# Feed-forward entry of a two-batch encoder layer: operand sums formed before the transpose instead of after it

## The chip, the cores and the metric

One core of a Trainium2 chip runs the whole layer for both batches in one launch. The metric is the device time of that launch in microseconds (us). The kernel before takes 1795.2 us (median of 3 runs, 1794.31 to 1796.43).

The engines named below: TensorE (PE in the profile) does matrix products and, by a product with an identity, transposes; VectorE (DVE), ScalarE (ACT) and GpSimd (POOL) work element by element; SyncE (SP) issues the transfers between the chip's memory (DRAM) and SBUF. TensorE writes into PSUM, which GpSimd does not read here. Each engine works through its own instructions in order.

## The reference, cut to what matters

Two batches of 512 tokens with 1024 features go through one layer: a mixer of two branches, an output projection `w_out` added to `x`, and then a feed-forward block. The change touches the seam between the projection and the feed-forward block:

```
x = x + (g_a * y_a + g_b * y_b) @ w_out[l]
h = _rmsnorm(x, norm_ffn_g[l])            # x * rsqrt(mean(x*x) + eps) * gain
gt, up = jnp.split(h @ w_gu[l], 2, axis=-1)
x = x + (jax.nn.silu(gt) * up) @ w_down[l]
```

All is float32. A product is made of three matmuls over a high and a low part: `hi*hi + hi*lo + lo*hi`, where `hi` is the value rounded to TensorE's short format and `lo` is the rest.

## The kernel before, in words

**The gate/up product.** `h @ w_gu` is done for both batches together by a scheme of seven products in place of eight (Strassen's, in Winograd's form). The transposed normalized rows are cut into four quadrants: the first and the second half of the features, for batch 0 (B11 and B21) and for batch 1 (called z0 and z1 in the code; z1 is B22). From them come the sums T1 = z0 - B11, T2 = B22 - T1, T3 = B22 - z0 and T4 = B21 - T2. The operands of the products are B11, B21, B22, T1, T2, T3 and T4, each held as a `hi` and a `lo` tile with features on the partitions. The weights of block `j` come in two loads of 512 KB, `graw` (A11 and A12) and `uraw` (A21 and A22); GpSimd forms the sums S1 to S4 from them, and ScalarE (`hi`) and VectorE (`lo`) split them. Both loads go into three shared buffers tagged `raw`.

**The order of the stages at this seam.**

1. `combine(1, ...)` makes the merged rows of batch 1, eight steps `j` with two products `pab` of 12 matmuls each. At steps 0, 2, 4 and 6 a hook calls `first_norm(t)` for row tile `t` (128 tokens) of batch 0: square and sum, the power -1/2 on GpSimd, scale the rows, transpose both halves on TensorE (`nt_f`), multiply with the gain while leaving PSUM (`nscf`), then `split` into B11 and B21. The gain stands per partition here, since the features are on the partitions after the transpose. `EF` puts the low part of this split on GpSimd.
2. `project(1, 0, ...)` multiplies with the first half of `w_out`'s columns (`pwo`).
3. A `Window` records operations with an engine, a cost, a rank and what they wait for, and writes them out in the order that its planner finds; later scheduling keeps that order. Recorded are: `w_project(t)` (second half of the columns, 24 matmuls for a row tile), `w_norm(t)` (norm, two transposes, gain, and T1, B22, T3 and T2 for batch 1), `w_combos(t)` (T2, T4 and T3 split), and `w_product(i)`, the first product and half of the next for weight blocks 0 and 1 (`pgA`).
4. `gate_up(j)` for the blocks: in block 0 and 1 `pgB` needs T1 whole, `pgC` T2 and then T3, `pgB` again B22, and `pgC` last T4.

In the window before the change a row tile's chain is: add the projection to `x` (L1447, VectorE), square and sum over 1024 features (L1457, ScalarE), L1459 (VectorE), power (L1461, GpSimd), scale 1024 features (L1462, VectorE), two transposes (TensorE), two multiplications by the gain out of PSUM (L1471, VectorE), two subtractions for T1 (L1479 and L1481: B11 exists only as `hi` and `lo`), T3 (L1485), T2 (L1487), T4 (L1494, L1495) and the splits of L1429 (ScalarE) and L1430 (GpSimd or VectorE, by the strings `ET1` to `ET4` and `EB22`).

Of the kernel before, what the change touches and what calls it, by code (L numbers as in the profile page):

```python
# [108 lines left out]
def trunk(ctx, tc, outs, x, w_in, w2, g2, w_uq, w_ukk, w_ukv, w_oab, w_out, w_gu, w_down,  # L109
          cols, fng, ident, te, to, mask2, reset, blk64, blk2):  # L110
# [1167 lines left out]
    B11, B21 = (operand(bp0, n) for n in ("B11", "B21"))  # L1278

    def first_norm(cp_, t):  # L1280
# [10 lines left out]
        for g, dst in enumerate((B11, B21)):  # L1291
            nc.vector.tensor_scalar_mul(h[g], xs[:, g], ss[:, 0:1])
# [3 lines left out]
            nc.vector.tensor_mul(sc, ps.rearrange("p (k t) -> p k t", k=KH),  # L1296
                                 cc(C_GFFN + g * KH, KH).unsqueeze(2).to_broadcast([P, KH, P]))
# [126 lines left out]
    COST = {nc.vector: ("V", 0.6), nc.gpsimd: ("G", 1.23)}  # L1424
    early, psb = {}, []

    def w_split(dst, t, src, rank, eng, *deps):
# [1 line left out]
        hi = W.op("A", 0.52, rank, lambda: nc.scalar.copy(dst()[0][:, :, ts], src()), *deps)  # L1429
        lo = W.op(*COST[eng], rank, lambda: eng.tensor_sub(dst()[1][:, :, ts], src(), dst()[0][:, :, ts]), hi)  # L1430
# [19 lines left out]
    def w_norm(t, old):  # L1450

        ts, xt, z = slice(t * P, (t + 1) * P), x2[4 + t], {}

        def square():
            z["ss"] = np_.tile([P, 1], F32, tag="nss", bufs=4, name=f"nssf1{t}")
            z["ht"] = np_.tile([P, D], F32, tag="nh", bufs=1, name=f"nhf1{t}")
            return nc.scalar.activation(z["ht"], xt, AF.Square, accum_out=z["ss"])  # L1457
        o = W.op("A", 1.04, 0, square, *psb[-1:], *old.get("tr", ()))
        o = W.op("V", 0.07, 0, lambda: nc.vector.tensor_scalar(z["ss"], z["ss"], 1.0 / D, RMS_EPS,  # L1459
                                                               op0=ALU.mult, op1=ALU.add), o)  # L1460
        o = W.op("G", 0.46, 0, lambda: nc.gpsimd.tensor_tensor(z["ss"], z["ss"], mhalf[:, :1], op=ALU.pow), o)  # L1461
        o = W.op("V", 0.66, 0, lambda: nc.vector.tensor_scalar_mul(z["ht"], xt, z["ss"]), o)  # L1462
        r = {"tr": [], "nsc": [], "z": z}

        def tr(g):
            z["ps", g] = bank(3, f"nt_f1{t}{g}")
            tr4(z["ps", g], lambda i: z["ht"][:, (g * 4 + i) * P:(g * 4 + i + 1) * P])

        def scale(g):
            z[g] = np_.tile([P, KH, P], F32, tag=f"nsc{g}", bufs=(4, 1)[g], name=f"nscf1{t}{g}")  # L1470
            return nc.vector.tensor_mul(z[g], z["ps", g].rearrange("p (k t) -> p k t", k=KH),  # L1471
                                        cc(C_GFFN + g * KH, KH).unsqueeze(2).to_broadcast([P, KH, P]))
        for g in range(2):
            r["tr"].append(W.op("T", 0.43, 0, lambda g=g: tr(g), o, *old.get("nsc", [])[g:g + 1]))
            r["nsc"].append(W.op("V", 0.6, 0, lambda g=g: scale(g), r["tr"][g], *(old.get("b22", ()) if g else ())))
# [375 lines left out]
```

## Time and profile before

| | |
|---|---|
| time, median of 3 runs | 1795.2 us (1794.31 to 1796.43) |
| the profiled execution's own time | 1793.97 us |
| its span in the trace | 1792.2 us |
| mean granted TensorE clock | 0.984 |

The page of the profile gives each engine's busy time over the span and cuts the span in 40 slices; a table of stretches gives the same for any piece of it. The list of waits says which engine stood idle for which; a timeline row gives start, duration, engine, line, operation, and in brackets the idle time just ahead of it with what ended it. A row on a line or a group gives minimum, median and maximum of its instructions' durations in ns. The seam that is changed lies between 1017 and 1173 us of the span. The rows themselves stand in the prediction, where they are used.

### The profile page before, as it was taken

To read this page: it belongs to the slowest core of one execution; us is meant where nothing else is said; L and a number is where in the kernel's file an instruction comes from. 1 tells how busy PE (TensorE), PEld (TensorE's weight loads), DVE (VectorE), ACT (ScalarE), POOL (GpSimd) and SP (SyncE) were. 2 spreads that over 40 slices of the span, in tenths; PEclk is the share of its full clock that TensorE was granted. 3 is DMA by queue.
4 is the path that set the end of the run, shared out by engine and by line. 5 is a ranking of instruction groups with operands and counts; after the bars stand their busy time and mean duration, and the time that the engine had idled before them with its cause. 6 is when DMAs were issued, how large, how long until landed. Compare 5 with 4: busy or idle time off the path is not lost.

```text
span 1792.2 us, 30028 instructions
## 1 busy us (share of the span) xinstructions
PE 1700.9 (95%) x11276; PEld 1327.8 (74%) x11276; DVE 1075.6 (60%) x1773; ACT 787.9 (44%) x1533; POOL 627.3 (35%) x984
## 2 busy tenths in 40 slices
PE   7999999999999997999999999699999999989997
PEld 6778766777777775666667877488888888868886
DVE  6734464636445365855566665955565465498657
ACT  6643424344433335666663432433333333245445
POOL 1121536274554736261012143833343333200006
PEclk9999999999999998999999999899999999999999
DMA  5473342434334344211267531123222222383442
GB/s 179 135 259 100 107 116 79 132 86 125 114 85 121 84 116 118 73 40 34 110 207 266 176 126 36 36 88 107 94 93 96 83 90 76 100 307 110 130 134 94
DMA packets 181233, 208.90 MB, mean 117 GB/s; under 512 B 102816, under 2 KB 106272, under 8 KB 181088
## 3 DMA queue, kind: packets, MB, share of 16 engines
q1 hardware_dynamic: 180224, 205.48, 36.3%
q8 instruction: 88, 1.44, 0.3%
q10 hardware_dynamic: 720, 0.98, 0.2%
q0 software_dynamic: 144, 0.52, 0.1%
q14 instruction: 57, 0.47, 0.1%
HBM read 147.70 MB, written 59.24 MB: 115 GB/s over the span
## 4 chain that ended last, share of the span: by engine, by line
PE 72%; DVE 9%; POOL 6%; DMA 6%; issue 3%; ACT 2%; SPq 1%; DVEq 0%; POOLq 0%; ACTq 0%
PE pgC L129 10%; PE pj_gt L129 8%; PE pgB L129 6%; PE pgA L129 6%; PE pj_rkv L129 4%; PE dx L129 4%; PE pwo L129 4%; PE pab L129 3%; PE s L129 2%; PE dy L129 2%; POOL el L966 2%; POOL lt L964 2%; PE sc L129 2%; PE pj_mla L129 2%; PE pav L129 2%
## 5 line engine op out<-in xcount | busy, mean ns | idle before, releaser
L964 POOL TENSOR_TENSOR lt<-lane,el 128x126 f32<-128x126 f32 (+22 forms) x248 | 94.1, 379 | 36.7 <-DMA lane<-nt_d 18.1
L966 POOL TENSOR_TENSOR el<-el,lt 128x126 f32<-128x126 f32 (+22 forms) x248 | 98.9, 399 | 19.0
L129 PE MATMUL pab<-yo,wab 128*128 128x512 f32 x384 | 96.5, 403 | 5.5 <-DVE wab L137 2.8
L129 PE MATMUL pj_gt<-h_hi,wlo_gt 128*128 128x512 f32 x240 | 98.4, 410 | 1.2 <-DVE wlo_gt L137 1.2
L129 PE MATMUL pj_gt<-h_lo,whi_gt 128*128 128x512 f32 x240 | 99.4, 414 | 0.0
L129 PE MATMUL pj_gt<-h_hi,whi_gt 128*128 128x512 f32 x240 | 99.0, 412 | 0.0
L129 PEld LDWEIGHTS pab<-yo,wab 128*128 128x128 f32 x384 | 71.7, 191 | 24.2 <-DVE wab L137 5.1
L1344 POOL TENSOR_TENSOR s<-uraw 128x512 f32<-128x512 f32 x22 | 29.3, 1334 | 154.3 <-DMA uraw<-in_w_gu 154.0
L129 PE MATMUL pwo<-woh,m 128*128 128x512 f32 x256 | 80.4, 390 | 0.0
L129 PE MATMUL pj_rkv<-h_hi,wlo_rkv 128*128 128x512 f32 x192 | 79.1, 412 | 0.0
L129 PE MATMUL pj_rkv<-h_hi,whi_rkv 128*128 128x512 f32 x192 | 78.6, 410 | 0.0
L129 PE MATMUL pj_rkv<-h_lo,whi_rkv 128*128 128x512 f32 x192 | 78.2, 407 | 0.0
L1720 POOL TENSOR_TENSOR x<-x,dp 128x512 f32<-128x512 f32 x4 | 6.3, 1593 | 177.5 <-DVE x L1719 177.5
L1412 DVE TENSOR_TENSOR p<-p,pgC 128x512 f32<-128x512 f32 x22 | 15.1, 687 | 82.3 <-PE pgC L129 82.3
L1053 ACT COPY sva<-s 64x128 f32<-64x128 f32 x64 | 16.5, 258 | 100.8 <-PE s L129 87.3
L129 PEld LDWEIGHTS pwo<-woh,m 128*128 128x128 f32 x256 | 48.1, 188 | 10.0
L1054 DVE COPY svb<-s 64x128 f32<-64x128 f32 x64 | 18.9, 295 | 60.5 <-ACT sva L1053 35.8
L775 DVE TENSOR_REDUCE mx<-sc 128x1 f32<-128x512 f32 x64 | 43.6, 687 | 15.7 <-PE sc L129 14.9
L129 PEld LDWEIGHTS pj_gt<-h_hi,wlo_gt 128*128 128x128 f32 x240 | 45.1, 188 | 9.9 <-DVE wlo_gt L137 1.7
L129 PEld LDWEIGHTS pj_gt<-h_hi,whi_gt 128*128 128x128 f32 x240 | 45.1, 188 | 8.9
L129 PEld LDWEIGHTS pj_gt<-h_lo,whi_gt 128*128 128x128 f32 x240 | 45.1, 188 | 8.6
L1354 POOL TENSOR_TENSOR s<-graw,uraw 128x512 f32<-128x512 f32 x22 | 29.2, 1325 | 63.8 <-DVE S_2l L137 5.0
(1563 smaller groups left out, 5458.4 us busy)
## 6 DMA issues: line engine op xcount, KB each, us to landing
graw<-in_w_gu SPq DMA_DIRECT2D x22, 512.0 KB, 3.6
uraw<-in_w_gu SPq DMA_DIRECT2D x22, 512.0 KB, 3.6
a_d<-a SPq DMA_DIRECT2D x21, 512.0 KB, 3.4
w<-in_w_down SPq DMA_DIRECT2D x42, 256.0 KB, 4.5
x<-in_x SPq DMA_DIRECT2D x16, 512.0 KB, 7.1
rwkv_in<-lut SPq DMA_DIRECT2D x32, 256.0 KB, 2.4
gate_d<-gtt SPq DMA_DIRECT2D x32, 256.0 KB, 2.4
wab<-in_w_oab SPq DMA_DIRECT2D x32, 256.0 KB, 3.8
```

Source lines behind the costliest of these rows:

```text
L129: pin(nc.tensor.matmul(out, lhsT, rhs, start=start, stop=stop, **kw), n if out.shape[0] > 64 else n / 2)
L775: nc.vector.tensor_reduce(mx, sc, axis=AX.X, op=ALU.min)
L964: eng.tensor_mul(lv, lane[:, s, s + 1:].unsqueeze(1).to_broadcast([P, m_, n]), el[:, 0:m_, s].unsqueeze(2).to_broadcast([P, m_, n]))
L966: eng.tensor_add(ev, ev, lv)
L1053: nc.scalar.copy(sva[HA, :, c], s2[HA])
L1054: nc.vector.tensor_copy(svb[HB, :, c], s2[HB])
L1344: vg(ES[min(j, 1)]).tensor_add(s1, a21, a22)
L1354: vg(ES[min(j, 1)]).tensor_sub(s3, a11, a21)
L1412: nc.vector.tensor_add(p1, p1, x_)
L1720: nc.gpsimd.tensor_add(xs(1, t, 1), xs(1, t, 1), p5[t])
```

## The change

The normalized rows are multiplied with the gain before they are transposed, in one VectorE instruction (row times its factor times gain). For that the gain comes as a new input `ffg`, the vector repeated on 128 rows; it is loaded into one of the three `raw` buffers. In `first_norm` the rows of batch 0 are also stored to DRAM (`n0_d`), and the transposed rows are split straight from PSUM, the low part on VectorE. In the window the sums T1 to T4 are formed of rows, not of transposed operands: T1 subtracts batch 0's row, read back from DRAM, in one instruction; each operand is then transposed by itself and split straight from PSUM. GpSimd keeps only the power. The squares are done in two halves, the first of which does not wait for the window's projection.

```diff
+R1, R2, RW, RP = (1, 1, 2), (3, 10, 14), 1, 3
-ET1 = 'ggvv'
-EF = 'gggg'
...
+    n0_d = [dram.tile([P, 2, S], F32, name=f"n0_d{t}") for t in range(4)]
+    gain = fwr[0].tile([P, D], F32, tag="raw", bufs=NRAW, name="ffg")
+    nc.sync.dma_start(gain, ffg)
...
         for g, dst in enumerate((B11, B21)):
-            nc.vector.tensor_scalar_mul(h[g], xs[:, g], ss[:, 0:1])
+            nc.vector.scalar_tensor_tensor(out=h[g], in0=xs[:, g], scalar=ss[:, 0:1], in1=gain[:, g * S:(g + 1) * S],
+                                           op0=ALU.mult, op1=ALU.mult)
+            nc.sync.dma_start(n0_d[t][:, g], h[g])
             ps = dn(f"nt_f0{t}{g}")
             tr4(ps, lambda i: h[g][:, i * P:(i + 1) * P])
-            sc = ld(f"nscf0{g}").rearrange("p (k t) -> p k t", k=KH)
-            nc.vector.tensor_mul(sc, ps.rearrange("p (k t) -> p k t", k=KH),
-                                 cc(C_GFFN + g * KH, KH).unsqueeze(2).to_broadcast([P, KH, P]))
-            split(dst[0][:, :, ts], dst[1][:, :, ts], sc, vg(EF[t]))
+            split(dst[0][:, :, ts], dst[1][:, :, ts], ps.rearrange("p (k t) -> p k t", k=KH))
...
+    def w_tr(t, name, i, src, dst, rank, late, *deps):
...
+        o = W.op("T", 0.44, rank, tr, *deps, *late, *[r[0] for r in trs[i][-1:]], *[r[1] for r in trs[i][-2:-1]])
+        hi = W.op("A", 0.6, rank, lambda: nc.scalar.copy(dst()[0][:, :, ts], z["v"]), o)
+        lo = W.op("V", 0.68, rank, lambda: nc.vector.tensor_sub(dst()[1][:, :, ts], z["v"], dst()[0][:, :, ts]), hi)
...
+    def w_row(t, g, rank, *deps):
...
+            z["w"] = np_.tile([P, S], F32, tag="w", bufs=2, name=f"n0{t}{g}")
+            return nc.sync.dma_start(z["w"], n0_d[t][:, g])
...
+        o = W.op("A", 0.6, 1, lambda: square(0))
+        o = W.op("A", 0.6, 0, lambda: square(1), psb[-1], o)
...
+        na = W.op("V", 0.7, 0, lambda: scale(0), o)
+        w, ld = w_row(t, 0, 0)
+        t1 = W.op("V", 0.7, 0, lambda: nc.vector.tensor_sub(w["w"], z["n"][:, 0], w["w"]), na, ld)
+        o1, _ = w_tr(t, "T1", 3, lambda: w["w"], lambda: T1, 0, (), t1)
+        nb = W.op("V", 0.7, R1[0], lambda: scale(1), o)
+        b22, _ = w_tr(t, "B22", 2, lambda: z["n"][:, 1], lambda: B22, R1[1], (), nb)
+        t3 = W.op("V", 0.7, R1[2], lambda: nc.vector.tensor_sub(z["n"][:, 0], z["n"][:, 1], z["n"][:, 0]), nb, t1)
+        t2 = W.op("V", 0.7, R1[2], lambda: nc.vector.tensor_sub(z["n"][:, 1], z["n"][:, 1], w["w"]), t3, b22, o1)
...
+        w, ld = w_row(t, 1, R2[2])
+        o = W.op("V", 0.7, R2[2] + t, lambda: nc.vector.tensor_sub(w["w"], w["w"], z["n"][:, 1]), ld, t2)
+        wbuf.append(w_tr(t, "T4", 3, lambda: w["w"], lambda: T4, R2[2] + t, (opened,), o)[0])
```

How the written order moves is shown at three places. First VectorE in the window, row tile 0 of batch 1 up to the projection of row tile 1 (`x_4` and `x_5` are the rows, `nssf` the factor, `n_12175` the row tile read back from DRAM, `n_12178` the normalized rows). Before:

```order
L1447 TENSOR_TENSOR x_4_10283<-x_4_10283,pwo_12180 128x512
L1459 TENSOR_SCALAR nssf_12214<-nssf_12214 128x1
L1462 TENSOR_SCALAR nhf_12215<-x_4_10283,nssf_12214 128x1024
L1471 TENSOR_TENSOR nscf_12242<-nt_f_12232,col 128x512
L1471 TENSOR_TENSOR nscf_12250<-nt_f_12237,col 128x512
L1479 TENSOR_TENSOR ntf_12252<-nscf_12242,B_11407 128x512
L1481 TENSOR_TENSOR ntf_12252<-ntf_12252,B_11408 128x512
L1447 TENSOR_TENSOR x_5_10284<-x_5_10284,pwo_12206 128x512
```

Now VectorE has at the same place:

```order
L1437 TENSOR_TENSOR x_4_10283<-x_4_10283,pwo_12180 128x512
L1479 TENSOR_TENSOR nssf_12177<-nssf_12177 128x1
L1480 TENSOR_SCALAR nssf_12177<-nssf_12177 128x1
L1486 SCALAR_TENSOR_TENSOR n_12178<-x_4_10283,nssf_12177,ffg 128x512
L1490 TENSOR_TENSOR n_12175<-n_12178,n_12175 128x512
L1486 SCALAR_TENSOR_TENSOR n_12178<-x_4_10283,nssf_12177,ffg 128x512
L1494 TENSOR_TENSOR n_12178<-n_12178 128x512
L1452 TENSOR_TENSOR T_11987<-nt_T_12246,T_11986 128x4x128
L1437 TENSOR_TENSOR x_5_10284<-x_5_10284,pwo_12220 128x512
```

No instruction of VectorE stands between the factor and T1 but the scaling itself; the gain's two passes out of PSUM and one of T1's subtractions are gone, and the split of T1's low part (L1452) has come to VectorE.

Second TensorE, from the end of row tile 1's projection on: `nt_T` and `nt_B` are the transposes for T1 and B22, and `x4` stands for four transposes of 128 x 128. Now:

```order
L128 MATMUL nt_T_12246<-idn,n_12175 128x128 x4
L124 MATMUL pwo_12220<-woh_12157,m_10823 128x512
L124 MATMUL pwo_12220<-wol_12158,m_10823 128x512
L124 MATMUL pwo_12220<-woh_12157,m_10824 128x512
L124 MATMUL pwo_12220<-woh_12157,m_10823 128x512
L124 MATMUL pwo_12220<-wol_12158,m_10823 128x512
L124 MATMUL pwo_12220<-woh_12157,m_10824 128x512
L128 MATMUL nt_B_12261<-idn,n_12178 128x128 x4
L124 MATMUL pwo_12267<-woh_12055,m_10823 128x512
```

Before, both transposes of a row tile stood together, for row tile 1 behind all of row tile 2's projection (`pwo_12255`):

```order
L129 MATMUL pwo_12255<-woh_12159,m_10823 128x512
L129 MATMUL pwo_12255<-wol_12160,m_10823 128x512
L129 MATMUL pwo_12255<-woh_12159,m_10824 128x512
L133 MATMUL nt_f_12293<-idn,nhf_12273 128x128 x4
L133 MATMUL nt_f_12299<-idn,nhf_12273 128x128 x4
```

Now T1's transpose stands behind 18 of the 24 matmuls of the next row tile's projection, and B22's behind all 24; twelve more groups of transposes, for T2, T3 and T4, follow between the matmuls of `pgA`, `pgB` and `pgC`.

Third SyncE's queue in the window (`wor` are rows of `w_out`, `n` the rows read back, `uraw` and `graw` the weights). Now:

```order
L1202 DMA wor_12161<-in_w_out 128x512
L1202 DMA wor_12165<-in_w_out 128x512
L1464 DMA n_12284<-n_d_11413 128x512
L1464 DMA n_12335<-n_d_11414 128x512
L1464 DMA n_12400<-n_d_11411 128x512
L1320 DMA uraw_12578<-in_w_gu 128x1024
L1464 DMA n_12478<-n_d_11412 128x512
L1320 DMA uraw_12686<-in_w_gu 128x1024
L1320 DMA graw_12792<-in_w_gu 128x1024
L1464 DMA n_12532<-n_d_11413 128x512
L1464 DMA n_12550<-n_d_11414 128x512
```

Before, `uraw` of block 0 was loaded early, right behind the two `graw` loads and ahead of step 3 of batch 0's combine:

```order
L1207 DMA wor_10834<-in_w_out 128x512
L1323 DMA graw_12173<-in_w_gu 128x1024
L1323 DMA graw_12175<-in_w_gu 128x1024
L1323 DMA uraw_12520<-in_w_gu 128x1024
L1169 DMA g_10925<-gate_d_86 128x1024
```

The gain now has that early place and buffer; `uraw` of block 0 has moved past the rest of the combine into the window, behind the reads of batch 0's rows, because it takes the gain's buffer once row tile 3 is scaled.

More of the change, by code (lines that the diff above doesn't have):

```diff
@@ L1438, in mms @@
             if k0 == 0:
-                z["ps"] = bank(1 + t % 2, f"pwo1{t}")
+                z["ps"] = bank(1, f"pwo1{t}")
             hi, lo = wo1[k0 // 2]
@@ L1448, in w_project @@
         return o[0]
[L1450 to L1459, printed above, removed]
-                                                               op0=ALU.mult, op1=ALU.add), o)
[L1461 to L1467, printed above, removed]
-        def scale(g):
[L1470 to L1475, printed above, removed]
-        def t1():
-            z["t1"] = np_.tile([P, KH, P], F32, tag="nt", bufs=3, name=f"ntf{t}")
-            return nc.vector.tensor_sub(z["t1"], z[0], B11[0][:, :, ts])
-        a = W.op("V", 0.6, 0, t1, r["nsc"][0], *(n[-3].get("T4", ()) if t > 2 else ()))
-        o = W.op("V", 0.6, 0, lambda: nc.vector.tensor_sub(z["t1"], z["t1"], B11[1][:, :, ts]), a)
-        r["T1"] = w_split(lambda: T1, t, lambda: z["t1"], 0, vg(ET1[t]), o)
-        b = w_split(lambda: B22, t, lambda: z[1], PRIOW, vg(EB22[t]), r["nsc"][1])
-        eng = vg(ET3[t])
-        d = W.op(*COST[eng], PRIOW, lambda: eng.tensor_sub(z[0], z[1], z[0]), r["nsc"][1], a)
-        eng2 = vg(ET2[t])
-        r["T2"] = W.op(*COST[eng2], PRIOW, lambda: eng2.tensor_sub(z["t1"], z[1], z["t1"]), *r["T1"], r["nsc"][1])
-        r["b22"], r["T3"] = (*b, d, r["T2"]), d
-        return r
@@ L1491, in w_combos @@
-    def w_combos(t, r):
-        ts, z, eng = slice(t * P, (t + 1) * P), r["z"], vg(ET4[t])
-        o = w_split(lambda: T2, t, lambda: z["t1"], 3 + t, nc.vector, r["T2"], opened)
-        for i, f in enumerate((lambda: eng.tensor_sub(z["t1"], B21[0][:, :, ts], z["t1"]),
-                               lambda: eng.tensor_add(z["t1"], z["t1"], B21[1][:, :, ts]))):
-            o = [W.op(*COST[eng], 4 if t == 0 else 14 + t, f, *o)]
-        r["T4"] = w_split(lambda: T4, t, lambda: z["t1"], 4 if t == 0 else 14 + t, nc.vector, *o)
-        w_split(lambda: T3, t, lambda: z[0], 10 + t, nc.vector, r["T3"], opened)
+    trs = {2: [], 3: []}
@@ L1535, in w_product @@
             copied.append(W.op("A", 0.48, 1, copy, *o, *copied[-1:]))
-    n, last, copied = [{}], [], []
+    n, last, copied = [], [], []
     fw = T2 = T3 = T4 = None
@@ L1541, in trunk @@
         last.append(w_project(t))
-        if t == 3:
-            opened = W.op(None, 0, 0, reopen, *last)
-            for i in range(3):
-                w_combos(i, n[i + 1])
-        n.append(w_norm(t, n[-1]))
-    w_combos(3, n[4])
+        n.append(w_norm(t))
+    opened = W.op(None, 0, 0, reopen, *last)
+    for f in (w_second, w_third):
+        for t in range(4):
+            f(t, *n[t])
     for i in range(2 * NE):
```

49 lines of the change are left out of this document (35 added, 14 removed).

## The prediction

> **What bounds the kernel now.** I read the page first, for the share of each engine; then a table of stretches, to find where TensorE is not full; then TensorE's list of waits and timeline in those stretches.
>
> ```profile
> span 1792.2 us, 30028 instructions
> PE 1700.9 (95%) x11276; PEld 1327.8 (74%) x11276; DVE 1075.6 (60%) x1773; ACT 787.9 (44%) x1533; POOL 627.3 (35%) x984
> ...
> core 0: us, PE busy (x) PEld busy (x) DVE busy (x) ACT busy (x) POOL busy (x), PEclk, DMA share, GB/s
> 1017.00:1051.30 34.30, 30.84 (x136) 24.03 (x136) 29.78 (x47) 16.49 (x35) 16.14 (x14) 0.95 0.41 131
> 1051.30:1098.70 47.40, 47.40 (x212) 38.83 (x211) 22.53 (x34) 11.71 (x21) 8.80 (x6) 1.00 0.26 83
> 1098.70:1172.70 74.00, 55.80 (x238) 44.04 (x237) 58.77 (x63) 28.64 (x50) 53.79 (x37) 0.88 0.10 29
> 1172.70:1560.00 387.30, 387.30 (x1710) 320.71 (x1709) 218.51 (x279) 131.64 (x224) 136.87 (x97) 1.00 0.28 94
> ```
>
> The kernel is bound by TensorE. Of the four stretches two are full at clock 1.00; the other two hold all of the change: the first norm (1017 to 1051), where TensorE idles 34.30 - 30.84 = 3.5 us, and the window (1098.7 to 1172.7), where it idles 18.2 us at a granted clock of 0.88. Behind 1172.7 TensorE runs without a gap for 387 us, so time gained ahead of it stays gained.
>
> ```profile
> PE pab L129 <- DVE wab L137: 2.6, 1, 2.6
> ...
> PE nt_f L133 <- DVE nhf L1462: 6.6, 3, 4.7
> PE pgB L129 <- ACT T L1429: 5.9, 1, 5.9
> PE pgB L129 <- DVE T L1430: 3.7, 1, 3.7
> ...
> 1028.23 0.63 PE L133 MATMUL nt_f<-idn,nhf 128*128 128x128 f32 x4 [0.79 <-DVE nhf L1292]
> 1046.84 4.60 PE L129 MATMUL pab<-yo,wab 128*128 128x512 f32 x12 [2.57 <-DVE wab L137]
> 1117.64 1.06 PE L133 MATMUL nt_f<-idn,nhf 128*128 128x128 f32 x8 [1.68 <-DVE nhf L1462]
> 1127.49 1.94 PE L133 MATMUL nt_f<-idn,nhf 128*128 128x128 f32 x8 [4.68 <-DVE nhf L1462]
> 1144.89 0.80 PE L129 MATMUL pgB<-T,S_0h 128*128 128x512 f32 x1 [5.91 <-ACT T L1429]
> ```
>
> Every wait is for VectorE or for a cast of ScalarE that follows VectorE. Why VectorE is late:
>
> ```profile
> L1430 DVE TENSOR_TENSOR T<-ntf,T x10: 674/1752/1777, 1123.2 to 1161.9; 128x512 fp32r<-128x512 f32 x10
> ...
> L1485 POOL TENSOR_TENSOR nscf<-nscf,nscf 128x512 f32<-128x512 f32 x4 | 6.9, 1735 | 6.3 <-ACT B L1429 3.9 <-DVE ntf L1479 2.3
> L137 POOL TENSOR_TENSOR B<-nscf,B 128x512 fp32r<-128x512 f32 x8 | 10.9, 1363 | 13.4 <-ACT B L136 13.4
> ...
> L1292 DVE TENSOR_SCALAR nhf<-x,nssf x8: 480/1489/1518, 1018.3 to 1044.1; 128x512 f32<-128x512 f32 x8
> L1296 DVE TENSOR_TENSOR nscf<-nt_f,col x8: 677/678/681, 1021.5 to 1056.0; 128x512 f32<-128x512 f32 x8
> ```
>
> The same subtraction takes VectorE 674 ns at best and 1752 ns in the median, while GpSimd is busy 53.79 of the window's 74 us. What reads PSUM (L1296) never stretches: 677 to 681 ns. So GpSimd's work slows VectorE's work on SBUF by 1.08 us an instruction.
>
> **What goes.** GpSimd loses 8 splits in the first norm and 20 instructions in the window (28 rows in all); it keeps powers, `g` and the weight sums. On VectorE 16 gain passes out of PSUM go, and 28 low-part splits read PSUM instead of SBUF, so they do not stretch. On the path, the first norm's cure is 0.79 + 2.57 us of waits, and the slow matmuls behind the second: 12 in 4.60 us, against 2.80 for the same twelve next:
>
> ```profile
> 1051.88 2.80 PE pab L129 x12
> ...
> 1102.81 0.45 PE nt_f L133 x4
> ...
> 1167.38 5.44 PE pgB L129 x24
> ```
>
> That is 0.79 + 2.57 + 1.80 = 5.2 us. Why the second wait should go: VectorE's `wab` split stood behind two `nhf` that GpSimd stretched (1489 against 480 ns); now it stands ahead of row tile 3's scaling, and no GpSimd split runs beside it. What takes its place: row tile 1's scaling now stands ahead of the split for step 1's weights. Walking VectorE's order from 1017.4 puts that split's end about 0.4 us behind TensorE's need. First stretch: 5.2 - 0.4 = **4.8 us**, with bounds of 0 (a new wait as large as the old) and 5.2.
>
> [...] The replaced L1292 has one tensor input; the new form has two, as in the last norm:
>
> ```profile
> L1638 DVE SCALAR_TENSOR_TENSOR x<-x,frs,fg x7: 743/746/751, 1779.6 to 1788.3; 128x512 f32<-128x512 f32 x7
> ```
>
> I take 0.75 us for each. [...] The measured median of 1489 ns decides: each becomes 0.74 us shorter.
>
> **The window: will TensorE be fed?** A row tile takes TensorE 24 matmuls at 5.44 / 24 = 0.227 us and two transpose groups at 0.45 us, 6.3 us. T1's transpose stands 0.45 + 18 x 0.227 = 4.5 us behind the end of its own projection. The chain to it:
>
> ```profile
> 1098.76 0.69 DVE L1447 TENSOR_TENSOR x<-x,pwo 128x512 f32<-128x512 f32 x1 [2.89 <-PE pwo L129]
> ...
> 1016.49 0.63 ACT L1288 ACTIVATE nhf<-x 128x512 f32<-128x512 f32 x1 [1.35 <-DVE x L1266]
> 1017.25 0.16 DVE L1289 TENSOR_TENSOR nssf<-nssf 128x1 f32<-128x1 f32 x1 [0.19 <-ACT nhf L1288]
> 1017.74 0.56 POOL L176 TENSOR_TENSOR nssf<-nssf,mhalf 128x1 f32<-128x1 f32 x1 [24.69 <-DVE nssf L175]
> 1018.33 0.49 DVE L1292 TENSOR_SCALAR nhf<-x,nssf 128x512 f32<-128x512 f32 x1
> ```
>
> Addition 0.75 with the hand-over; from a 512-wide square's start to the scaling, as in the first norm, 1018.33 - 1016.49 = 1.84; scaling 0.75; subtraction 0.68: 4.0 us, half a microsecond inside 4.5. The first square, the power and batch 0's row (loaded some 5 us earlier) lie beside other work. VectorE's load per row tile is eight instructions of 0.6 to 0.75 us plus 0.3, 5.5 us of 6.3. So the three waits for `nhf` (6.6 us) and, with T1 split as it goes, those for `pgB` (5.9 and 3.7 us) should go. If every SBUF instruction were still stretched by 1.08 us, the tile would take VectorE about 11 us and this cover would be gone.
>
> What is late next is the weights. `uraw` of block 0 waits for row tile 3's last scaling, which the walk puts at 1122.3 (window start unmoved). From issue to use:
>
> ```profile
> 1157.24 0.33 SPq L1323 DMA_DIRECT2D uraw<-in_w_gu  x1
> ...
> 1161.48 1.68 POOL L1344 TENSOR_TENSOR s<-uraw 128x512 f32<-128x512 f32 x1 [0.84 <-DMA uraw<-in_w_gu]
> ```
>
> 4.24 us, so GpSimd forms S1 from 1126.6 to 1128.2, the cast ends at 1128.9, and TensorE comes to it at 1128.3: **0.6 us** of wait. Transposes of T2, T3 and T4 and the rest of `pgA` cover its low part. GpSimd's four sums, 1.3 to 1.7 us each with VectorE's splits between, end at 1133.3; then block 1's `uraw` can take `graw`'s buffer: issue 1133.3, use 1137.5, S1 of block 1 cast at 1139.4, its low part (stretched once by GpSimd) at 1141.1. TensorE, held 0.8 us by T3's splits for a PSUM bank, is there at 1138.4: waits of **1.05 and 1.25 us**. T4's rows for tiles 2 and 3 stand in SyncE's queue behind that `uraw` and a `graw` that waits for VectorE; they land near 1140 and VectorE comes to them at 1143. With 0.15 us at T1 of tile 0 the new waits are 0.15 + 0.6 + 0.8 + 1.05 + 1.25 = 3.85 us.
>
> TensorE's work between the two ends of the window: 204 matmuls x 0.227 = 46.2 us, now with 20 transpose groups in place of 8, 20 x 0.45 = 9.0 (5.4 us of it new). New length 46.2 + 9.0 + 3.85 = 59.1 against 74.0: **14.9 us**. Bounds: no new wait gives 18.8; the weights' loads at the slowest time the page shows for 512 KB (7.1 us from issue to landing, against 3.6) add 3.5 us twice and slow matmuls behind them, 1.8 us each as after the 2.57 us wait: 14.9 - 7 - 3.6 = 4.3.
>
> ```profile
> graw<-in_w_gu SPq DMA_DIRECT2D x22, 512.0 KB, 3.6
> ...
> x<-in_x SPq DMA_DIRECT2D x16, 512.0 KB, 7.1
> ```
>
> The eight stores and eight loads of 256 KB cost SyncE 0.33 us each to issue. In the first norm a store holds what is behind it until its row is scaled, but the `wab` and gate loads behind wait for later VectorE work in any case: nothing. DMA share there is 0.41, in the window 0.10.
>
> [...] After waits of 2.57, 4.68 and 5.91 us TensorE's next matmuls are slow; after 1.68 us the eight transposes took 1.06 us, no slower than elsewhere. I therefore cost the new waits (1.25 us at most) with no slow matmuls. [...]
>
> **Sum.** 4.8 + 14.9 = 19.7 us from the profiled execution's 1794.0 us (1792.2 of span and 1.8 around it): 1774.3. The median of the runs is 1.2 us above that execution, so the time shown should be **1775.5 us**.
>
> **Rivals.**
> - *The weights become the bound.* The gain's buffer makes both `uraw` loads wait in turn. For: the loads were early and are now on the path. Against: 3.6 us in the median. With the slow loads, 4.8 + 4.3 = 9.1 us of gain: 1786. Half-way cases lie from 1779 on. Chance 0.22.
> - *The first norm gives nothing back*, because the longer scaling stands ahead of `wab` splits at each step. For: 29.78 of 34.30 us of VectorE are busy there. Against: the stretched 1489 ns. Gain 14.9: 1780. Chance 0.07.
> - *Nothing waits anew*: 5.2 + 18.8 = 24 us: 1771. Chance 0.08.
> - *The gain is given back* in `gate_up` by loads that come no earlier than before: about 1795. Against: 387 us without a gap. Chance 0.03.
> - *Slower: VectorE becomes the bound in the window.* It takes over the splits; were all of its SBUF instructions stretched, a row tile would take it 11 us against 6.3 for TensorE, 4 x 4.7 = 19 us lost, and some eight more in the T4 and S stage than the walk counts another 8.6: 1775.5 + 27.4 = 1803. It decides from some 18 stretched instructions beyond the walk's on (19.7 / 1.08). Against: GpSimd keeps four powers of 0.56 us and eight sums here. Chance 0.05.
>
> **How the numbers follow.** Forecast 0.55, for 1772 to 1779. The range takes in the first three rivals but for the slowest of the loads' cases: 1769 to 1788 leaves out some 0.12. A measurement of this kernel tells a change from none above about 0.2% (3.6 us). Faster by more than that: 0.55 + 0.22 + 0.07 + 0.08 = 0.92, less 0.02 for the slowest loads, 0.90; within: 0.05; slower: 0.05.
>
> **What would show it.** Right: VectorE's subtractions near 0.68 us in the window; waits for `nhf` and for T gone; TensorE's window about 59 us long, with its longest waits for S1 of blocks 0 and 1. Wrong: waits over 2.5 us for S1 with slow matmuls behind (loads), VectorE without idle time and TensorE waiting at each `nt_T` (VectorE the bound), or a wait for `wab` in the first norm as long as the old one.

## The result and the profile after

The changed kernel took 1774.03 us (median of 4 runs, 1772.35 to 1776.99) against 1795.82 us (4 runs, 1794.31 to 1797.56): a ratio of 0.988, 95% interval 0.9862 to 0.9898, or 21.5 us. Measured once more (6 runs against 23) the ratio was 0.9906, 0.9891 to 0.9921, or 16.9 us.

Two landmarks make the stretches comparable between kernels whatever happened ahead of them. The **first stretch** runs from VectorE's fifth addition of `pwo` to `x` (just ahead of the first norm) to the last `pab` matmul. The **window** runs from the first addition of the window's own projection to the first `pgC` matmul with `a22_0`. The table of stretches for before and for the changed kernel (start and end, length, then each engine's busy time and its instructions, granted clock, DMA share, GB/s):

```profile
core 0: us, PE busy (x) PEld busy (x) DVE busy (x) ACT busy (x) POOL busy (x), PEclk, DMA share, GB/s
1015.77:1076.94 61.17, 57.70 (x256) 45.90 (x255) 43.76 (x67) 22.96 (x45) 23.66 (x19) 0.97 0.36 115
1098.76:1172.65 73.89, 55.69 (x236) 43.94 (x235) 58.72 (x63) 28.64 (x50) 53.79 (x37) 0.88 0.10 28
1172.65:1792.20 619.55, 600.64 (x2641) 494.76 (x2639) 393.60 (x553) 237.64 (x423) 170.19 (x123) 1.00 0.34 115
```

```profile
1010.97:1068.32 57.35, 56.10 (x256) 44.75 (x255) 37.25 (x67) 22.39 (x45) 13.94 (x11) 1.00 0.49 159
1090.13:1149.01 58.88, 56.58 (x284) 45.55 (x282) 48.72 (x75) 26.86 (x50) 21.01 (x17) 1.00 0.22 66
1149.01:1770.50 621.49, 603.60 (x2642) 497.12 (x2640) 394.95 (x554) 237.69 (x423) 169.98 (x123) 0.99 0.35 115
```

The window is 15.0 us shorter (73.89 to 58.88), the first stretch 3.8 (61.17 to 57.35): 18.8 us in what was changed. The spans differ by 21.7. The other 2.9 us lie where nothing of the work changed: ahead of the first stretch the changed kernel is 4.8 us earlier (1010.97 against 1015.77), behind the window it takes 1.9 us longer. That is taken up below.

TensorE's list of waits between 1011 and 1149 us of the changed kernel (what waited, for what, us in total, times, longest) is what is left. Length less busy time, TensorE stood idle for 3.5 + 18.2 us in the two stretches before and for 1.25 + 2.3 us now:

```profile
PE pgB L124 <- ACT S_1h L131: 1.2, 1, 1.2
PE pab L124 <- DVE wab L132: 1.2, 1, 1.2
PE pgB L124 <- DVE S_1l L132: 0.5, 1, 0.5
PE nt_T L128 <- DVE T L1452: 0.3, 1, 0.3
PE pgB L124 <- ACT S_0h L131: 0.2, 1, 0.2
```

VectorE's instructions by line in the window up to 1130 us (count, then minimum/median/maximum in ns, first and last start) show why. What had a median of 1752 ns at the low parts of `T` now has one of 680, and none of these is far from its minimum:

```profile
L1486 DVE SCALAR_TENSOR_TENSOR n<-x,nssf,ffg x8: 740/748/752, 1092.7 to 1113.9; 128x512 f32<-128x512 f32 x8
L1490 DVE TENSOR_TENSOR n<-n,n x4: 691/692/693, 1093.5 to 1112.7; 128x512 f32<-128x512 f32 x4
L1452 DVE TENSOR_TENSOR T<-nt_T,T x11: 673/680/693, 1095.5 to 1129.0; 128x512 fp32r<-128x512 f32 x11
```

Not every instruction of the window is free of the stretch. From 1118.5 us on GpSimd forms the weight sums, and beside them low parts of `S` take up to 1.64 us and the subtractions for T4 (L1505) up to 1.24 us.

### The profile page after: what moved, and what is told of

Read it like the earlier page. It is cut to its first block, busy times and chain, and to the rows that moved or that the text cites. A ratio compares the mean times of both kernels' runs of the same rounds, so it can differ in the third digit from the quotient of the medians.

```text
span 1770.5 us, 30142 instructions
## 1 busy us (share of the span) xinstructions
PE 1700.2 (96%) x11324; PEld 1327.5 (75%) x11324; DVE 1061.5 (60%) x1785; ACT 788.0 (45%) x1541; POOL 583.4 (33%) x956
## 4 chain that ended last, share of the span: by engine, by line
PE 70%; DVE 8%; DMA 8%; POOL 7%; issue 3%; ACT 3%; SPq 1%; POOLq 0%; DVEq 0%; ACTq 0%
PE pgC L124 10%; PE pj_gt L124 7%; PE pgB L124 7%; PE pgA L124 6%; PE dx L124 4%; PE pj_rkv L124 4%; PE pwo L124 4%; PE pab L124 3%; PE s L124 2%; POOL el L961 2%; POOL lt L959 2%; PE dy L124 2%; PE sc L124 2%; PE pj_mla L124 2%; PE pav L124 2%
## 5 line engine op out<-in xcount | busy, mean ns | idle before, releaser
L1049 DVE COPY svb<-s 64x128 f32<-64x128 f32 x64 | 18.8, 294 | 61.1 <-ACT sva L1048 37.6
L1177 POOL TENSOR_TENSOR g<-g 128x512 f32<-128x512 f32 x16 | 24.9, 1555 | 84.6 <-DVE g L1175 66.1
```

The costliest lines, as they stand in the source:

```text
L1049: nc.vector.tensor_copy(svb[HB, :, c], s2[HB])
L1177: nc.gpsimd.tensor_add(g_[:, 0], g_[:, 0], g_[:, 1])
```

## The experiments

The theory at this point: GpSimd's work on SBUF stretches VectorE's, so that taking it off the stretch feeds TensorE; the rest of the gain comes from fewer passes; late weights and one `wab` split are what is left. Lengths in us from the table of stretches of each run's profile, so of one execution each; ratio to before with its interval.

| kernel | ratio (95%) | fifth addition at | first stretch | window |
|---|---|---|---|---|
| before | 1 | 1015.77 | 61.17 | 73.89 |
| changed | 0.988 (0.9862-0.9898) | 1010.97 | 57.35 | 58.88 |
| changed, again | 0.9906 (0.9891-0.9921) | 1016.21 | 56.98 | 59.89 |
| first norm alone | 0.9985 (0.9974-0.9996) | 1016.63 | 56.31 | 73.96 |
| before without GpSimd | 0.9965 (0.995-0.998) | 1017.93 | 57.30 | 67.11 |
| before, GpSimd cut | 1.0022 (1.0005-1.0039) | 1014.44 | 57.93 | 80.03 |
| changed, first norm on GpSimd | 0.9908 (0.9886-0.993) | 1016.17 | 58.70 | 58.49 |
| changed, 40 narrow on GpSimd | 0.9919 (0.9898-0.9941) | 1018.13 | 57.26 | 62.89 |
| changed, 9 wide on GpSimd | 0.9959 (0.9937-0.9981) | 1011.86 | 57.24 | 66.81 |
| changed, no store | 0.9895 (0.9877-0.9912) | 1021.56 | 55.90 | 58.49 |
| changed, stores by GpSimd | 0.9901 (0.9883-0.9918) | 1014.32 | 57.78 | 58.61 |
| changed, stores held behind | 0.9899 (0.9885-0.9914) | 1014.00 | 57.64 | 58.67 |
| changed, stores twice | 0.9909 (0.9885-0.9934) | 1019.71 | 57.88 | 58.59 |
| changed, early weights | 0.9906 (0.989-0.9923) | 1014.40 | 56.88 | 62.18 |

**The changed kernel again.** No edit.

> The changed kernel once more, for a second profile and a tighter ratio. The profiled executions differ by 21.7 us of span, but only 18.5 us of that arise between the first addition of the projection (x<-x,pwo, 991.4 us before and 986.7 us after) and the end of the window; 4.7 us stand ahead of it, where both kernels have the same instructions. Theory 'clock by chance': those 4.7 us are a matter of the single execution; here the first addition falls anywhere from 986 to 992 us, while first stretch plus window are again 18 to 19 us shorter than before. Rival 'the change reaches back' (its new load of the gain and another order of transfers ahead of the first norm): the first addition stands at 986.7 +- 0.5 again. Ratio 0.987 to 0.990 by both.

The fifth addition came at 1016.21 us (the first at 991.79). Over all 14 profiles it stands between 1010.97 and 1021.56: the three kernels without the new input lie from 1014.44 to 1017.93, the eleven with it on both sides of that. So the 4.8 us ahead of the stretch are a matter of the single execution, not of the change. First stretch and window were 4.2 and 14.0 us shorter than before, 18.2 together; the window held 3.4 us at half clock here (mean clock 0.97).

**The first norm alone**, in the kernel before:

```
-            nc.vector.tensor_scalar_mul(h[g], xs[:, g], ss[:, 0:1])
+            nc.vector.scalar_tensor_tensor(out=h[g], in0=xs[:, g], scalar=ss[:, 0:1], in1=gain[:, g * S:(g + 1) * S],
+                                           op0=ALU.mult, op1=ALU.mult)
+            nc.sync.dma_start(n0_d[t][:, g], h[g])
...
-            split(dst[0][:, :, ts], dst[1][:, :, ts], sc, vg(EF[t]))
+            split(dst[0][:, :, ts], dst[1][:, :, ts], ps.rearrange("p (k t) -> p k t", k=KH))
```

> The kernel before with only the first norm of the change (gain in the rows, rows stored but never read, split from PSUM on VectorE). My theory: the first stretch loses 3.9 us (waits of 0.79 and 2.57 us and 1.8 us of slow matmuls, against a new wait of 1.2 us), the window stays at 74 us: 1792 us, ratio 0.998. Rival 'the first norm gives nothing by itself': 1795.8, ratio 1.000. Rival 'it also gains what stands ahead of it' (4.7 us): 1787, ratio 0.995.

The first stretch lost 4.9 us (56.31), a little more than expected, since only 0.15 us of new wait came up here; the window stayed at 73.96. So the window's gain owes nothing to the new first norm. In time the kernel was 0.15% faster, 0.04 to 0.26: 2.7 us, with the stretch's 4.9 just outside.

**The kernel before without GpSimd**: `ET1` to `ET4`, `EB22` and `EF` set to `'vvvv'`.

> The kernel before with its six strings set to VectorE: GpSimd does none of the 8 splits of the first norm and none of the window's 20 instructions, all passes stay. My theory (GpSimd's work on SBUF stretches VectorE's): the subtractions of VectorE fall to 0.68 us; a row tile then costs VectorE 0.68 + 1.0 + 2 x 0.68 + 2 x 0.68 + 4 x 0.68 + 0.3 = 7.4 us against 6.3 of TensorE, so a wait of about 1 us a row tile stays, and the window falls from 74 to some 64 to 68 us; first stretch 2 to 4 us shorter: 1782 to 1788 us. Rival 'the passes cost, not GpSimd': VectorE takes 28 instructions more at its old 1.3 to 1.75 us each: slower than before, 1805 or more. Rival 'all of the gain is GpSimd's absence': as the change, 1774.

First stretch 57.30, window 67.11: 3.9 + 6.8 = 10.7 us, although VectorE took 28 more instructions. The scaling `L1292` fell from a median of 1489 to 482 ns; three of the eight, which met GpSimd's work on the gate (`g`, L1182), still took 1.5 us. The window still waits for VectorE:

```profile
PE pgB L129 <- ACT T L1429: 4.8, 1, 4.8
PE nt_f L133 <- DVE nhf L1462: 4.0, 1, 4.0
PE pgA L129 <- DVE a_1l L1519: 1.7, 1, 1.7
```

By the stretches GpSimd's absence alone is worth more than half of the gain. In time it was 6.2 us (3.6 to 9.0), which leaves the 10.7 out. Behind the window the profiled execution took 624.54 us against 619.55 before, for the same work; why the time gained less over all runs is not shown.

GpSimd makes VectorE late in a second way, which the prediction does not name: the power stands in GpSimd's queue behind its splits and sums. In the window VectorE waited for the power for 4.8 us before (four waits) and for 1.1 us here. So the 6.8 us are not the stretch alone. The 8.2 us from 67.11 to 58.88 come from the rest: no gain pass, one subtraction for T1, and the order that goes with it. These were not tried apart.

**Narrow and wide work on GpSimd, in the changed kernel.** 40 subtractions of 128 x 128 whose result nobody reads, and in another kernel 9 of 128 x 512; every other engine's order is the same to the row.

```
+NX = 10
...
+    dum = np_.tile([P, P], F32, name="dum")
...
+        for i in range(NX):
+            W.op("G", 0.4, 1, lambda i=i: nc.gpsimd.tensor_sub(dum, B11[0][:, i % 4, :P].bitcast(F32), B11[1][:, i % 4, :P].bitcast(F32)), o)
```

```
+NX = 3
...
+        for i in range(NX if t < 3 else 0):
+            W.op("G", 1.4, 1, lambda i=i: nc.gpsimd.tensor_sub(mt[1][1][:, 4 * (i % 2):4 * (i % 2) + 4, ts], B11[0][:, :, ts].bitcast(F32), B11[1][:, :, ts].bitcast(F32)), o)
```

> The changed kernel with 40 additional subtractions of 128 x 128 on GpSimd in the window (10 for a row tile, into a scratch tile nobody reads); every other engine's order is the same to the row. My theory (GpSimd's work on SBUF stretches VectorE's work on SBUF and not its work out of PSUM): L1486, L1490, L1494 and L1495, at 0.69 to 0.75 us now, rise to 0.9 to 1.5 us in the mean; L1452 and L1437, which read PSUM, stay at 0.68; TensorE waits for VectorE again and the window is 3 to 12 us longer: 1777 to 1786. Rival 'only the number of passes matters': nothing stretches, 1774 within 1 us.

> The changed kernel with 9 additional subtractions of 128 x 512 on GpSimd in the window (3 for each of row tiles 0 to 2, into a part of batch 1's merged rows that is read no more); every other engine's order is the same to the row. The run with 40 narrow ones (128 x 128, 641 ns each) kept GpSimd busy for 33 of 40 us and stretched VectorE's L1486, L1490, L1494 and L1495 by only 0.14 to 0.19 us each. Theory 'one instruction of VectorE waits for one instruction of GpSimd at most, so the stretch goes by the length of GpSimd's instruction': here, with GpSimd busy for some 12 to 16 of 40 us only, the instructions that meet one become 1.2 to 1.8 us long, the others stay at 0.69 to 0.75; TensorE waits 1 to 4 us at nt_T, the window is 60 to 63 us. Rival 'the stretch goes by GpSimd's share of busy time': no more than 0.1 us each, the window stays at 58.5 to 59.5.

VectorE by line with the narrow ones (scaling, T1's subtraction, low part of `T`), then GpSimd's group (busy us, mean ns, idle time before), then the first 30 us of the window:

```profile
L1488 DVE SCALAR_TENSOR_TENSOR n<-x,nssf,ffg x8: 871/942/945, 1099.7 to 1124.7; 128x512 f32<-128x512 f32 x8
L1494 DVE TENSOR_TENSOR n<-n,n x4: 825/828/828, 1100.7 to 1123.3; 128x512 f32<-128x512 f32 x4
L1454 DVE TENSOR_TENSOR T<-nt_T,T x4: 676/678/691, 1103.2 to 1125.6; 128x512 fp32r<-128x512 f32 x4
```

```profile
L1491 POOL TENSOR_TENSOR dum<-B,B 128x128 f32<-128x128 f32 x40 | 25.6, 641 | 2.8
```

```profile
1097.20:1127.20 30.00, 26.68 (x134) 21.20 (x133) 25.26 (x40) 10.01 (x21) 25.45 (x41) 1.00 0.11 30
```

The same three views with the wide ones:

```profile
L1487 DVE SCALAR_TENSOR_TENSOR n<-x,nssf,ffg x8: 744/1766/1772, 1093.5 to 1123.0; 128x512 f32<-128x512 f32 x8
L1494 DVE TENSOR_TENSOR n<-n,n x4: 692/1632/1649, 1095.3 to 1121.8; 128x512 f32<-128x512 f32 x4
L1453 DVE TENSOR_TENSOR T<-nt_T,T x6: 681/684/692, 1099.2 to 1128.2; 128x512 fp32r<-128x512 f32 x6
```

```profile
L1491 POOL TENSOR_TENSOR m<-B,B 128x512 fp32r<-128x512 f32 x9 | 14.0, 1576 | 0.0
```

```profile
1090.92:1120.92 30.00, 24.44 (x111) 19.39 (x110) 26.59 (x33) 7.72 (x17) 16.42 (x13) 0.94 0.07 22
```

With GpSimd busy for 25.45 of 30 us in narrow pieces, VectorE's work on SBUF is 0.14 to 0.19 us longer in the median; with GpSimd busy for 16.42 us in wide ones, those that meet one (nine of L1487 and L1494) are 0.94 to 1.02 longer. In row tile 3, which has no additional work in the wide run, the same instructions take 0.69 to 0.75 us. The split out of PSUM does not move in either (678 and 684 ns, against 680 in the changed kernel). The rival, that GpSimd's share of busy time counts, is out.

The window grew by 4.0 and 7.9 us, and only the second is the stretch alone: VectorE's wait for the power is 1.2 us with the wide ones, as in the changed kernel, but 3.2 us with the narrow ones, since the ten of one row tile stand ahead of the next one's power in GpSimd's queue. I had expected a smaller window with the wide ones (60 to 63); some 2 us of the excess is slow matmuls (TensorE busy for 58.63 us of the window, 56.58 in the changed kernel). In time only the kernel with the wide ones is clear of the changed kernel.

**GpSimd's work cut, in the kernel before**: most subtractions of 128 x 512 become four of 128 x 128 each, by this helper.

```
+    def cut(eng, out, a, b):
+        if eng is nc.vector:
+            return eng.tensor_sub(out, a, b)
+        for k in range(4):
+            r = eng.tensor_sub(out[:, k], a[:, k], b[:, k])
+        return r
```

> The kernel before with most of GpSimd's subtractions of 128 x 512 in the first norm and in the window (8 splits, and the splits and sums that stand with B22, T1, T2 and T3 of row tiles 0 to 3) cut into four of 128 x 128 each; the two-step T4 sums stay whole. On the changed kernel narrow ones stretched VectorE by 0.14 to 0.25 us an instruction and wide ones by 1.0. If the stretch goes by the length of GpSimd's instruction in the kernel before too: VectorE's scaling L1292 falls from a median of 1489 ns to below 800, T1's subtractions too; the wait for wab in the first norm shrinks and the stretch (fifth addition to the end of pab) goes from 61.2 to 57 to 59 us. In the window GpSimd itself gets longer (4 x 0.64 = 2.6 us in place of 1.4 to 1.7 for each of some 16), so GpSimd may become what TensorE waits for: window 68 to 78 us. Rival 'only GpSimd's busy time counts': VectorE's instructions stay stretched, both stretches get longer.

The scaling's line on VectorE, and the two stretches:

```profile
L1299 DVE TENSOR_SCALAR nhf<-x,nssf x8: 472/562/689, 1017.0 to 1041.3; 128x512 f32<-128x512 f32 x8
```

```profile
1014.44:1072.37 57.93, 56.28 (x257) 45.06 (x256) 39.14 (x67) 22.73 (x45) 29.89 (x43) 1.00 0.37 120
1094.19:1174.22 80.03, 57.73 (x235) 45.12 (x234) 56.86 (x63) 29.00 (x50) 62.38 (x79) 0.87 0.09 27
```

In the first norm, where GpSimd has time to spare, this alone brought 3.2 us of the change's 3.8: the scaling fell from 1489 to 562 ns while GpSimd was busy for 6 us longer. In the window GpSimd had no time to spare (62.38 us busy now, 53.79 before): VectorE waited 12.4 us for the power there, 4.8 before. The window got 6.1 us longer, 2 more than the worst I had expected.

**The first norm back on GpSimd, in the changed kernel**: a copy out of PSUM by VectorE, the low part on GpSimd.

```
-            split(dst[0][:, :, ts], dst[1][:, :, ts], ps.rearrange("p (k t) -> p k t", k=KH))
+            sc = ld(f"nscf0{g}").rearrange("p (k t) -> p k t", k=KH)
+            nc.vector.tensor_copy(sc, ps.rearrange("p (k t) -> p k t", k=KH))
+            split(dst[0][:, :, ts], dst[1][:, :, ts], sc, nc.gpsimd)
```

> The changed kernel, but in the first norm the transposed rows are copied out of PSUM by VectorE and their low part is formed by GpSimd, as before. My theory: L1290's scaling is stretched from 0.75 to about 1.5 us again, the wait for wab comes back at 2 to 3 us with slow matmuls behind: 3 to 5 us slower than the changed kernel, 1777 to 1779; the window does not change. Rival 'the order of VectorE cured it, not GpSimd's absence': the first stretch stays within 0.5 us, 1774.

Neither fits: 58.70, that is 1.4 to 1.7 us back and not 3 to 5. VectorE's order had moved with the edit, and the stretch came back, but mostly on other instructions. Of the eight scalings only two took 1.78 us (the median stayed at 743 ns); of the 14 `wab` splits, 0.68 us each in the changed kernel, four took 1.37 to 1.69 us. VectorE was busy for 44.82 us with as many instructions as in the changed kernel's 37.25, and TensorE waited 2.0 us for `wab`. In time the kernel cannot be told from the changed one.

**Batch 0's rows: no store, another queue, held behind, twice.** Without stores the window reads the gain's rows in their place, so T1 to T4 are other numbers there.

```
-            nc.sync.dma_start(n0_d[t][:, g], h[g])
...
-            return nc.sync.dma_start(z["w"], n0_d[t][:, g])
+            return nc.sync.dma_start(z["w"], ffg[:, g * S:(g + 1) * S])
```

> The changed kernel without the eight stores of batch 0's rows; the window reads the gain's rows from DRAM in their place, so T1 to T4 are not what they should be, with the same loads. VectorE's, ScalarE's and TensorE's order is the same to the row. Theory 'stores delay the gate's load' (it landed 4.9 us after its issue behind two stores, against 3.5 to 3.8 otherwise): the landing falls to 3.7 us, the wait of 1.19 us for wab goes, 1.0 to 1.3 us faster than the changed kernel. Rival 'VectorE's order' (the scaling ahead of the split, as the prediction has it): the wait stays at 1.2 us.

> The changed kernel with the eight stores issued by GpSimd in place of SyncE; all else in the same order. If what delays the gate's load is that it stands behind the stores in one queue: the load lands in 3.7 us and the wait of 1.19 us for wab goes, 1 us faster than the changed kernel. If it is the traffic alone: the landing stays at 4.5 to 5 us and the wait at 1 us or more. If the issue on GpSimd gets in the way of its powers: the scaling waits longer, and the wait grows.

> The changed kernel with the stores of batch 0's rows held behind the gate's load of the same step in SyncE's queue. Without any store the waits for wab in the first norm went from 0.7 to 1.2 us to none and the stretch (fifth addition to the end of pab) from 57.0 to 57.4 us to 55.9; with the stores on GpSimd's queue the gate's load still landed in 4.6 us and the wait was 1.6. Theory 'the traffic of the two stores ahead of it delays the gate's load': behind it they cost it nothing, it lands in 3.7 us, the wait goes, the stretch is 56 to 56.4 us: 1 us faster than the changed kernel. Rival 'they delay whatever load is behind them': a wab load lands late in its place and the wait stays, 57 to 57.5 us. Where a store holds a buffer that the next row tile's squares need, it is longer still.

> The changed kernel with each of the eight stores issued twice (the second to rows in DRAM nobody reads). Theory 'the stores' traffic delays the loads of the first norm' (no store: no wait and 55.9 us for the stretch; one: waits of 0.7 to 1.2 us and 56.9 to 57.4): the gate's load behind four stores of 256 KB lands 1 to 2 us later than behind two (5.5 to 7 us), and the wait for wab grows to 2 to 3.5 us, the stretch to 58.5 to 61. Rival 'the wait comes from VectorE's order and the run without stores was chance': the stretch stays at 57 to 57.5.

SyncE's, VectorE's and TensorE's timeline in the changed kernel around the wait that is left in the first norm:

```profile
1031.56 0.99 SPq L1292 DMA_DIRECT2D n_d<-nhf  x2
1032.82 0.32 SPq L1164 DMA_DIRECT2D g<-gate_d  x1
...
1032.11 0.68 DVE L1179 SCALAR_TENSOR_TENSOR m<-g,m 128x512 fp32r<-128x512 f32 x1
...
1037.80 0.69 DVE L1175 SCALAR_TENSOR_TENSOR g<-g,pab 128x512 f32<-128x512 f32 x1 [2.62 <-DMA g<-gate_d]
1038.41 0.68 DVE L1179 SCALAR_TENSOR_TENSOR m<-g,m 128x512 fp32r<-128x512 f32 x1
1039.01 0.68 DVE L132 TENSOR_TENSOR wab<-wab,wab 128x512 fp32r<-128x512 f32 x1
...
1039.75 3.06 PE L124 MATMUL pab<-yo,wab 128*128 128x512 f32 x12 [1.19 <-DVE wab L132]
```

The gate's load is issued when VectorE's `m` has freed its buffer (1032.11 + 0.68), behind two stores. It lands at 1037.8, 4.9 us later, while VectorE stands in its order at `g`, with the `wab` split that TensorE needs two places behind. From issue to landing the six loads of the gate in this stretch take 3.5/3.8/4.9 us (minimum, median, maximum) in the changed kernel and 3.4/3.7/3.8 us without stores.

Without stores the wait is gone and TensorE runs the whole first stretch, 55.90 of 55.90 us. The changed kernel and its variants with the first norm as it is (again, narrow, wide, early weights) took 56.88 to 57.35, so the stores cost 1.0 to 1.5 us here, by one profile without them. The price depends on what stands around them: the first norm alone stores the same rows and took 56.31. How they cost it is less clear. Issued by GpSimd they delay a gate's load as much (4.6 us), so that does not need one queue; but the wait of 1.6 us stands at a later `wab` split, ahead of which VectorE had waited 2.4 us for TensorE and not for a load. Held behind the gate's load (VectorE's order moved by some rows with that) they left a wait of 1.5 us for a `wab` split, though not for the rival's reason: no late load stands there, but two scalings just ahead that took 2.43 us together, one of them stretched to 1.77. Twice as many made it 57.88 with 1.5 us of waits, less than the 58.5 to 61 expected; their second half was partly issued behind the load. With one profile each, neither the way nor the dose is shown. In time neither of the two variants that keep the result can be told from the changed kernel; no version was found that beats it.

**Early weights**: the window scales with rows of `x` in place of the gain, so batch 1's normalized rows are other numbers; the gain's buffer comes free behind the first norm.

```
-                                                  in1=gain[:, g * S:(g + 1) * S], op0=ALU.mult, op1=ALU.mult)
+                                                  in1=x2[0][:, g * S:(g + 1) * S], op0=ALU.mult, op1=ALU.mult)
```

> The changed kernel, but the window scales with rows of x in place of the gain, so that the gain's buffer comes free behind the first norm and the first uraw is loaded some 70 us earlier; batch 1's normalized rows are not what they should be. My theory (late weights make the waits for S0 and S1, 0.22 + 1.21 + 0.52 us, and the 0.31 us at a transpose): they go, 1.5 to 2.3 us faster than the changed kernel. Rival 'VectorE is as late as the weights there': the waits move to T3 or T4 and no more than 0.5 us is gained. Rival 'a single instruction of GpSimd in the row tiles stretches VectorE': the sums now run beside the row tiles, the window gets 1 to 3 us longer.

My theory fell; the last rival holds, a little beyond its 1 to 3 us. The waits for S0 and S1 went, as expected, but GpSimd's sums now run in row tile 3. VectorE's and GpSimd's timeline there:

```profile
1113.44 1.63 POOL L1342 TENSOR_TENSOR s<-s,graw 128x512 f32<-128x512 f32 x1
1113.83 1.25 DVE L1479 TENSOR_TENSOR nssf<-nssf 128x1 f32<-128x1 f32 x1
...
1116.25 1.28 POOL L1348 TENSOR_TENSOR s<-graw,s 128x512 f32<-128x512 f32 x1
1116.31 1.77 DVE L1486 SCALAR_TENSOR_TENSOR n<-x,nssf,x 128x512 f32<-128x512 f32 x1 [0.44 <-POOL nssf L1482]
...
1118.95 1.72 PE L128 MATMUL nt_T<-idn,n 128*128 128x128 f32 x8 [1.83 <-DVE n L1490]
```

An addition of one column takes 1.25 us where it takes 0.16 alone, and the scaling 1.77. TensorE waits 1.83 us and its clock falls behind that (0.50 from 1119.21 us on, for 3.41 us): 62.18 us, 3.3 longer. In time the kernel cannot be told from the changed one (0.9906, as in the changed kernel's second measurement). The gain's buffer, which makes the weights late, keeps the sums out of the row tiles. Early weights with the sums held back were not tried.

## Why the prediction came out right, and where it did not

**The window (14.9 us predicted, 15.0 in the first profile, 14.0 in the second).** Its length was given as 59.1 us; it is 58.88, 58.5 to 58.7 in the variants that leave it alone, and 59.89 in the second profile. The walk's dates hold: with the window's start 8.63 us earlier, the first `uraw` was issued at 1114.67 + 8.63 = 1123.3 (predicted 1122.3), the second at 1124.98 + 8.63 = 1133.6 (1133.3). The waits came where they were placed, and summed to 2.26 us in place of 3.85: 0.22 us for S1 of block 0, 0.31 at the transpose held by a split of T, 1.21 and 0.52 for S1 of block 1. Against 0.6, 0.8, 1.05 and 1.25; the largest miss is the last, since the low part came 1.2 us behind its cast and not 1.7. What the waits gave back, TensorE's own work took: 56.58 us busy against 46.2 + 9.0 = 55.2. Two terms that were off by 1.6 and 1.4 us cancel, so the length hit better than its parts, which is luck.

**The first stretch (4.8 us predicted, 3.8 and 4.2 measured).** The cure worked as priced: 0.79 + 2.57 us of waits and 1.8 us of slow matmuls went. The step that failed is the one on the stores, "the `wab` and gate loads behind wait for later VectorE work in any case: nothing". The gate's load does wait for VectorE's `m`, but with the stores its flight is longer and the stretch takes 1.0 to 1.5 us more than without them. The new wait that I did foresee, 0.4 us at the split for step 1, behind the scaling, was 0 in the first profile and 0.16 in the second.

**GpSimd stretches VectorE.** Shown from both sides: taken away in the kernel before, VectorE's instructions shrink (10.7 us of the stretches, not all of it by the stretch, since the power comes earlier too), and put back in the changed one in wide pieces they grow again (+7.9). The price of "1.08 us an instruction" was right for the wide instructions of this kernel and is not a constant: in narrow pieces it is 0.14 to 0.19. What the prediction left out is GpSimd's queue, in which the power waits: its chain counts the power as undisturbed, which held because the change took the other work out of that queue too (VectorE's waits for it fell from 4.8 to 1.2 us). The slower rival, VectorE as the bound, did not come up, because in the row tiles GpSimd kept only the powers; the run with nine wide instructions more (+7.9 us) shows what decides it.

**The scaling.** 745 to 748 ns in both places, as taken from the last norm. Undisturbed it is the slower form: the replaced one took 1489 ns in the median beside GpSimd, but 482 ns in the kernel before without GpSimd.

**The clock.** In the first profile the waits of up to 1.21 us brought no slow matmuls, as assumed: 1.00 in both stretches, and so in the five variants that leave the window alone. In the second profile of the same kernel, 3.41 us at half clock came behind them, TensorE was busy for 58.02 us in place of 56.58, and the window was 1.0 us longer. The assumption held by luck in part; the last section shows on what it depends.

**The sum.** 19.7 us predicted, 18.2 to 18.8 measured in the stretches, 21.5 and 16.9 in time. The terms were 0.9 to 1.5 us too large together. That the first time still came out 1.5 us below the 1775.5 forecast is chance: in the first pair of profiles the untouched parts gave 4.8 us ahead and took 1.9 behind, and nothing in the prediction stood for that.

## What to carry to other kernels

Where VectorE is late, look at the spread of one instruction's durations before counting its work: a median far above the minimum, with GpSimd busy beside it (here 1752 against 674 ns), is worth curing. Three ways did it here: the operand read from PSUM (678 and 684 ns for the low parts of `T`, with additional work on GpSimd beside them), the work taken off GpSimd (482 ns for the scaling, from 1489), and, in the first norm, where GpSimd had time to spare, its instructions cut narrow (562 ns; in the window, where it had none, the cut made the stretch 6.1 us longer). Look also at what short work, here the power, stands in GpSimd's queue behind long work (VectorE waited for it for 4.8 us in the window before, 1.2 now). Price what an early transfer sets off (here sums on GpSimd) and not only the wait that it removes. Compare stretches between landmarks, not spans, when the effect is about 1%: the part ahead of the change alone moved by 10 us between executions.
